# Rotary embedding on one core: which 1/32 of the data the SyncE queue carries, and how the rotation is written

## The chip, the cores and the metric

The kernel runs on one core of one Trainium2 chip. The metric is the device time of one execution in microseconds; the time quoted for a kernel is the median of its runs.

The engines that matter here are VectorE (DVE in the profile), which does all the arithmetic of the rotation, ScalarE (ACT), which evaluates the sines, GpSimd (POOL), which does no arithmetic but queues the large transfers, and SyncE (SP), which queues four small ones. TensorE (PE) is not used.

## The reference

The input `x` is float32 of shape 8 x 8 x 1024 x 64: 64 heads (batch times heads) of 1024 rows with 64 columns, 16.78 MB. Each row is rotated by angles that depend only on its position:

```python
half = x.shape[-1] // 2                     # 32
angles = np.outer(positions, freqs)         # 1024 x 32
cos, sin = np.cos(angles), np.sin(angles)
x_first, x_second = x[:, :, :, :half], x[:, :, :, half:]
out_first  = x_first * cos - x_second * sin
out_second = x_first * sin + x_second * cos
return np.concatenate([out_first, out_second], axis=-1).astype(np.float32)
```

The output is as large as the input, so an execution reads 16.78 MB and writes 16.78 MB of device memory (HBM).

## The kernel before, in words

**Tiles.** The 64 heads are cut into 8 tiles of 8 heads. A tile fills 128 partitions: partition `chunk * 8 + head` holds 64 rows (`C`) of one head, 4096 elements. The loads that GpSimd queues cast float32 to bf16 on the way in (an `xt` tile is 1 MB in on-chip memory and 2 MB in HBM); the stores that it queues cast bf16 back to float32 on the way out.

**The edge.** Two whole heads, 0 and 1 (`edge = 2`), are left out of GpSimd's transfers. SyncE loads them as float32 at the start (`xf`, L75, two transfers of 256 KB), with another layout: 8 consecutive rows (`R`) on each partition. ScalarE casts them to bf16 (`x0`, L130). Because of the other layout they need a second pair of sine and cosine tables (`sin_r`, `cos_r`), made from a second load of the positions (`pos_r`, L125). Their result `last` is float32 and leaves on SyncE's queue (L179), as the last two transfers of the program. Tile 0 therefore lacks two of its eight heads: `moves` yields six transfers of 16 partitions each for it, in and out, and its buffer is cleared first (L83) since VectorE computes on all 128 partitions.

**Loads.** GpSimd queues, in the order tile 1, tile 2, the six pieces of tile 0, tiles 3 to 6, and tile 7 in two halves of 32 rows: 14 transfers (L89). All loads have a buffer of their own. A load that is to use a completion semaphore a second time waits for the earlier transfer on it, and there are eight of them for GpSimd's transfers: the loads of tiles 3 and 4 wait for tiles 1 and 2.

**Stores held back.** A do-nothing instruction on GpSimd (L149) depends on the first half of tile 7. GpSimd's queue is in order, so no store is queued before that half has landed.

**Tables.** VectorE spreads the positions and frequencies over the partitions (L93, L94), multiplies them to turns and reduces these to less than one turn (L101 to L107); ScalarE makes `sin` and `cos` (L111 to L115) in bf16. `sin_c` has two copies per row, the second negated by VectorE (L112).

**Rotation.** Three VectorE instructions of 128 x 4096 elements per tile, in which `swap` reads the two halves of each row in exchanged order:

```python
v.tensor_mul(out=t,  in0=xt, in1=sin_c)                # L142
v.tensor_mul(out=ot, in0=xt, in1=cos_c, broadcast)     # L143
v.tensor_add(out=ot, in0=ot, in1=swap(t))              # L145
```

The scheduler puts the L142 of the next tile between L143 and L145 of a tile. In program order the tiles go 1, 0, 2, ..., 7. The tables of the edge are made after the third tile in the source; the scheduler moved their first instruction, which needs `pos_r`, ahead of the first L145. GpSimd queues a store after each tile (L155, 13 transfers).

**The end.** SyncE's two stores of the edge wait for every earlier transfer but GpSimd's last store (the `clobber_nop` list).

Of the kernel before, what the change touches and what calls it, by code (L numbers as in the profile page):

```python
# [9 lines left out]
@with_exitstack  # L10
def kernel(
    ctx: ExitStack,
    tc: tile.TileContext,
    x: bass.AP,
    freqs: bass.AP,
    positions: bass.AP,
    out: bass.AP,
):
    nc = tc.nc
    f32 = mybir.dt.float32  # L20
    bf16 = mybir.dt.bfloat16
    i32 = mybir.dt.int32
    Act = mybir.ActivationFunctionType
    Alu = mybir.AluOpType

    b, h, seq, d = x.shape
    bh = b * h
    half = d // 2
    P = 128
    twopi = 2 * math.pi  # L30
    head = seq * d

    C = 64
    R = seq // P
    chunks = seq // C
    G = P // chunks
    edge = 2  # L40
    run = C * d
    ntiles = bh // G
    assert chunks * C == seq and G * chunks == P and bh % G == 0 and R * P == seq and chunks <= 32

    singles = ctx.enter_context(tc.tile_pool(name="singles", bufs=1))
    xpool = ctx.enter_context(tc.tile_pool(name="xin", bufs=ntiles))
    opool = ctx.enter_context(tc.tile_pool(name="xout", bufs=ntiles))
    tpool = ctx.enter_context(tc.tile_pool(name="tmp", bufs=2))

    def moves(t, tile_, g, lo=0, hi=run):
        if g:
            yield (bass.AP(tensor=t.tensor, offset=t.offset + g * G * head + lo,
                           ap=[[run, chunks], [head, G], [1, hi - lo]]), tile_[:, lo:hi])
            return
        for i in range(edge, G):
            yield (bass.AP(tensor=t.tensor, offset=t.offset + i * head, ap=[[run, chunks], [1, run]]),
                   tile_[i:P:G])

    def hbm_head(t, i):
        return bass.AP(tensor=t.tensor, offset=t.offset + i * head, ap=[[R * d, P], [1, R * d]])

    v = nc.vector
    words = mybir.dt.size(positions.dtype) // 4
    const = singles.tile([P, C * words + half], i32)
    v.memset(const, 0)  # L70
    pos_i = const[:, :C * words]
    fr = const[:, C * words:].bitcast(f32)
    xf = singles.tile([P, edge, R, d], f32)
    for i in range(edge):
        nc.sync.dma_start(out=xf[:, i], in_=hbm_head(x, i))  # L75
    nc.scalar.dma_start(
        out=pos_i[0:P:G].bitcast(positions.dtype),
        in_=bass.AP(tensor=positions.tensor, offset=positions.offset, ap=[[C, chunks], [1, C]]))
    nc.scalar.dma_start(out=fr[0:P:32], in_=freqs[None, :].to_broadcast([P // 32, half]))


    xts = [xpool.tile([P, run], bf16, name="xt") for g in range(ntiles)]
    v.memset(xts[0], 0.0)  # L83
    order = [1, 0] + list(range(2, ntiles))
    for g in order:
        cuts = [0, run] if g < ntiles - 1 else [0, run // 2, run]
        for lo, hi in zip(cuts, cuts[1:]):
            for src, dst in moves(x, xts[g], g, lo, hi):
                nc.gpsimd.dma_start(out=dst, in_=src)  # L89
    half_pi = singles.tile([P, 1], f32)  # L90
    nc.gpsimd.memset(half_pi, math.pi / 2)  # L91

    v.stream_shuffle(pos_i, pos_i, [i // G * G for i in range(32)])  # L93
    v.stream_shuffle(fr, fr, [0] * 32)  # L94
    fturn = singles.tile([P, 1, half], f32)
    v.tensor_scalar_mul(out=fturn[:, 0, :], in0=fr, scalar1=1.0 / twopi)

    def tables(pos_f, n, copies, name):

        turns = singles.tile([P, n, half], f32, name=f"turns{name}")  # L100
        v.tensor_mul(out=turns, in0=pos_f.to_broadcast([P, n, half]),  # L101
                     in1=fturn.to_broadcast([P, n, half]))
        whole = singles.tile([P, n, half], f32, name=f"whole{name}")
        magic = 1.5 * 2.0 ** 23
        v.tensor_scalar(out=whole, in0=turns, scalar1=magic, scalar2=magic,  # L105
                        op0=Alu.add, op1=Alu.subtract)
        v.tensor_sub(out=turns, in0=turns, in1=whole)  # L107

        sin = singles.tile([P, n, 2, half], bf16, name=f"sin{name}")
        cos = singles.tile([P, n, copies, half], bf16, name=f"cos{name}")  # L110
        nc.scalar.activation(out=sin[:, :, 0], in_=turns, func=Act.Sin, scale=twopi)  # L111
        v.tensor_scalar_mul(out=sin[:, :, 1], in0=sin[:, :, 0], scalar1=-1.0)  # L112

        nc.scalar.activation(out=whole, in_=turns, func=Act.Abs)  # L114
        nc.scalar.activation(out=cos, in_=whole[:, :, None, :].to_broadcast([P, n, copies, half]),  # L115
                             func=Act.Sin, scale=-twopi, bias=half_pi)
        return sin, cos

    pos_f = singles.tile([P, C, 1], f32)
    v.tensor_copy(out=pos_f, in_=pos_i.rearrange("p (c w) -> p c w", w=words)[:, :, :1])  # L120
    sin_c, cos_c = tables(pos_f, C, 1, "c")


    pos_r = singles.tile([P, R, words], i32)
    tc.keep_in_program_order(nc.scalar.dma_start(  # L125
        out=pos_r.bitcast(positions.dtype),
        in_=bass.AP(tensor=positions.tensor, offset=positions.offset,
                    ap=[[R, P], [1, R], [1, 1]])))
    x0 = singles.tile([P, edge, R * d], bf16)
    tc.keep_in_program_order(nc.scalar.copy(out=x0, in_=xf.rearrange("p e r d -> p e (r d)")))  # L130

    def swap(ap):

        part, rows, pair, cols = ap.ap
        return bass.AP(tensor=ap.tensor, offset=ap.offset + half,
                       ap=[part, rows, [-half, 2], cols])

    def rotate(xt):
        flat = "p c two h -> p (c two h)"
        ot = opool.tile([P, C, 2, half], bf16, name="ot")  # L140
        t = tpool.tile([P, C, 2, half], bf16, name="t")
        v.tensor_mul(out=t.rearrange(flat), in0=xt, in1=sin_c.rearrange(flat))  # L142
        v.tensor_mul(out=ot, in0=xt.rearrange("p (c two h) -> p c two h", two=2, h=half),  # L143
                     in1=cos_c.to_broadcast([P, C, 2, half]))
        v.tensor_add(out=ot, in0=ot, in1=swap(t))  # L145
        return ot


    nc.gpsimd.keepalive_nop(ins=[nc.gpsimd.lower_ap(xts[-1][:, :run // 2])])  # L149

    stored = []
    for i, g in enumerate(order):
        ot = rotate(xts[g])
        for dst, src in moves(out, ot.rearrange("p c two h -> p (c two h)"), g):
            tc.keep_in_program_order(nc.gpsimd.dma_start(out=dst, in_=src))  # L155
        stored.append(ot)
        if i == 2:
            pos_rf = singles.tile([P, R, 1], f32)
            v.tensor_copy(out=pos_rf, in_=pos_r[:, :, :1])  # L159
            sin_r, cos_r = tables(pos_rf, R, 2, "r")  # L160

    flat = [P, edge, R * d]
    last = singles.tile(flat, f32)
    t = tpool.tile([P, C, 2, half], bf16, name="t").rearrange("p c two h -> p (c two h)")
    t = t[:, :edge * R * d].rearrange("p (n e) -> p n e", n=edge)
    for o, w in ((t, sin_r), (last, cos_r)):
        v.tensor_mul(out=o, in0=x0,  # L167
                     in1=w.rearrange("p r two h -> p (r two h)")[:, None, :].to_broadcast(flat))
    rows = "p n (r two h) -> p (n r) two h"
    v.tensor_add(out=last.rearrange(rows, two=2, h=half), in0=last.rearrange(rows, two=2, h=half),  # L170
                 in1=swap(t.rearrange(rows, two=2, h=half)))


    sp = nc.sync
    sp.keepalive_nop(ins=[sp.lower_ap(cos_r)])
    for done in [xf, const, pos_r] + stored[:-1]:
        sp.clobber_nop(outs=[sp.lower_ap(done)])
    for i in range(edge):
        tc.keep_in_program_order(sp.dma_start(out=hbm_head(out, i), in_=last[:, i]))  # L179
    sp.clobber_nop(outs=[sp.lower_ap(stored[-1])])  # L180
    for i in range(edge - 1):
        sp.clobber_nop(outs=[sp.lower_ap(last[:, i])])


# [28 lines left out]
```

## Time and profile before

| | us |
|---|---|
| median of 3 runs | 90.85 (90.83 to 91.07) |
| time of the profiled execution | 91.07 |
| its span, first to last instruction | 89.0 |
| VectorE busy | 66.6 (75%), 44 instructions |
| ScalarE busy | 9.4 (11%), 8 instructions |
| GpSimd busy (issuing transfers) | 14.2 (16%), 32 instructions |
| packets of GpSimd's queue, share of 16 DMA engines' span | 90.8% |
| HBM read / written | 16.79 MB / 16.78 MB |

The profiled execution lasted 2.07 us longer than its span: what lies before the first and after the last instruction. It was also the slowest of the three runs, 0.22 us above the median. In the page, "GB/s" counts the bytes that arrive: a load that casts to bf16 counts at half of what it reads from HBM, a store at what it writes. The share of busy time is a mean over the whole span, and the kernel has a load stage and a store stage with different limits, so it is read by stretches of time.

### The profile page before, as it was taken

The numbers are of one execution on the slowest core, as the hardware profiler recorded it, in microseconds if no ns is written. First come the engines' busy times: TensorE is split into PE (matmuls) and PEld (weight loads), VectorE is DVE, ScalarE is ACT, GpSimd is POOL, SyncE is SP. The second block draws the span as 40 slices with busy tenths as digits, with TensorE's granted clock in tenths as the row PEclk, the third lists the DMA queues.
The fourth block names the chain that finished last, engine by engine and source line by source line (L and its number), as shares of the span: only waits on it lengthen the run. The fifth ranks groups of instructions, "written<-read, shape, count | busy, mean of one in ns | idle before, by whom it ended". The sixth has DMA issues, their size and how long they took to land.

```text
span 89.0 us, 169 instructions
## 1 busy us (share of the span) xinstructions
DVE 66.6 (75%) x44; ACT 9.4 (11%) x8; POOL 14.2 (16%) x32
## 2 busy tenths in 40 slices
DVE  4414993769009679999999999999999999993000
ACT  0500006993000320000000000000000000000000
POOL 5580020650000000000961101001002002002000
DMA  2999999999999999999799999998895895899993
GB/s 23 298 159 195 217 210 214 210 203 229 216 207 221 214 214 221 203 210 195 276 354 442 435 413 449 427 420 361 354 361 228 354 376 214 354 420 405 442 351 150
DMA packets 3304, 25.45 MB, mean 286 GB/s; under 512 B 664, under 2 KB 680, under 8 KB 1448
## 3 DMA queue, kind: packets, MB, share of 16 engines
q0 software_dynamic: 2544, 24.38, 90.8%
q1 hardware_dynamic: 576, 1.05, 3.6%
q10 hardware_dynamic: 184, 0.02, 0.3%
HBM read 16.79 MB, written 16.78 MB: 377 GB/s over the span
## 4 chain that ended last, share of the span: by engine, by line
DVE 41%; DMA 34%; issue 13%; POOL 2%; DVEq 1%; POOLq 0%
DMA xt<-in_x_dram 34%; DVE ot L145 18%; DVE ot L143 17%; DVE t L142 5%; POOL xt L89 1%; DVEq L208 1%; DVE t L167 1%; POOL half_pi L91 0%; POOLq L197 0%
## 5 line engine op out<-in xcount | busy, mean ns | idle before, releaser
L143 DVE TENSOR_TENSOR ot<-xt,cosc 128x4096 bf16<-128x4096 bf16 x8 | 18.3, 2283 | 0.9 <-ACT cosc L115 0.9
L142 DVE TENSOR_TENSOR t<-xt,sinc 128x4096 bf16<-128x4096 bf16 x8 | 18.3, 2284 | 0.0
L145 DVE TENSOR_TENSOR ot<-ot,t 128x4096 bf16<-128x4096 bf16 x8 | 18.3, 2282 | 0.0
L155 POOL DMA_DIRECT2D out_dram<-ot x13 | 6.6, 512 | 54.8 <-DVE ot L145 54.8
L89 POOL DMA_DIRECT2D xt<-in_x_dram x14 | 7.3, 538 | 11.1 <-DMA xt<-in_x_dram 9.3
L159 DVE CAST pos_rf<-pos_r 128x8 f32<-128x8 int32 x1 | 0.2, 170 | 4.4 <-DMA pos_r<-in_positions_dram 4.4
L111 ACT ACTIVATE sinc<-turnsc 128x2048 bf16<-128x2048 f32 x1 | 1.9, 1909 | 10.1 <-DVE turnsc L107 10.1
L94 DVE LOAD_MASK_SELECT const<-const x1 | 0.0, 14 | 3.1 <-DMA const<-in_freqs_dram 3.1
L101 DVE TENSOR_TENSOR turnsc<-pos_f,fturn 128x2048 f32<-128x2048 f32 x1 | 2.3, 2293 | 0.0
L107 DVE TENSOR_TENSOR turnsc<-turnsc,wholec 128x2048 f32<-128x2048 f32 x1 | 2.3, 2293 | 0.0
L112 DVE TENSOR_SCALAR sinc<-sinc 128x2048 bf16<-128x2048 bf16 x1 | 0.7, 694 | 2.0 <-ACT sinc L111 2.0
L83 DVE MEMSET xt<- 128x2048 uint32 x1 | 1.8, 1765 | 0.4 <-issue 0.4
L115 ACT ACTIVATE cosc<-wholec,half_pi 128x2048 bf16<-128x2048 f32 x1 | 2.0, 2002 | 0.1
L114 ACT ACTIVATE wholec<-turnsc 128x2048 f32<-128x2048 f32 x1 | 1.9, 1895 | 0.0
L167 DVE TENSOR_TENSOR last<-x,cosr 128x1024 f32<-128x1024 bf16 x1 | 1.2, 1225 | 0.8 <-ACT cosr L115 0.8
L111 ACT ACT_TABLE_LOAD x1 | 1.3, 1283 | 2.7 <-issue 2.7
L111 ACT ACTIVATE sinr<-turnsr 128x256 bf16<-128x256 f32 x1 | 0.4, 416 | 9.3 <-DVE turnsr L107 9.3
L105 DVE TENSOR_SCALAR wholec<-turnsc 128x2048 f32<-128x2048 f32 x1 | 1.2, 1226 | 0.0
L170 DVE TENSOR_TENSOR last<-last,t 128x1024 f32<-128x1024 f32 x1 | 1.2, 1215 | 0.0
L130 ACT CAST x<-xf 128x1024 bf16<-128x1024 f32 x1 | 1.0, 1028 | 0.0
L93 DVE LOAD_MASK_SELECT const<-const x1 | 0.0, 14 | 1.2 <-DMA const<-in_positions_dram 1.2
L70 DVE MEMSET const<- 128x160 int32 x1 | 0.2, 192 | 0.8 <-PEq L197 0.8
(16 smaller groups left out, 4.5 us busy)
## 6 DMA issues: line engine op xcount, KB each, us to landing
out_dram<-ot POOLq DMA_DIRECT2D x7, 2048.0 KB, 6.8
xt<-in_x_dram POOLq DMA_DIRECT2D x6, 1024.0 KB, 13.7
out_dram<-ot POOLq DMA_DIRECT2D x6, 256.0 KB, 7.6
xt<-in_x_dram POOLq DMA_DIRECT2D x2, 512.0 KB, 24.5
xt<-in_x_dram POOLq DMA_DIRECT2D x6, 128.0 KB, 13.5
xf<-in_x_dram SPq DMA_DIRECT2D x2, 256.0 KB, 2.9
out_dram<-last SPq DMA_DIRECT2D x2, 256.0 KB, 5.6
const<-in_positions_dram ACTq DMA_DIRECT2D x1, 8.0 KB, 3.2
```

Source lines behind the costliest of these rows:

```text
L83: v.memset(xts[0], 0.0)
L89: nc.gpsimd.dma_start(out=dst, in_=src)
L101: v.tensor_mul(out=turns, in0=pos_f.to_broadcast([P, n, half]), in1=fturn.to_broadcast([P, n, half]))
L107: v.tensor_sub(out=turns, in0=turns, in1=whole)
L111: nc.scalar.activation(out=sin[:, :, 0], in_=turns, func=Act.Sin, scale=twopi)
L114: nc.scalar.activation(out=whole, in_=turns, func=Act.Abs)
L115: nc.scalar.activation(out=cos, in_=whole[:, :, None, :].to_broadcast([P, n, copies, half]), func=Act.Sin, scale=-twopi, bias=half_pi)
L142: v.tensor_mul(out=t.rearrange(flat), in0=xt, in1=sin_c.rearrange(flat))
L143: v.tensor_mul(out=ot, in0=xt.rearrange("p (c two h) -> p c two h", two=2, h=half), in1=cos_c.to_broadcast([P, C, 2, half]))
L145: v.tensor_add(out=ot, in0=ot, in1=swap(t))
L155: tc.keep_in_program_order(nc.gpsimd.dma_start(out=dst, in_=src))
L167: v.tensor_mul(out=o, in0=x0, in1=w.rearrange("p r two h -> p (r two h)")[:, None, :].to_broadcast(flat))
```

## The change

The edge is cut differently, and with it the rotation is written in another way.

- SyncE no longer carries two whole heads. It loads the first 16 rows of every partition of tile 0 at the start (`x0`, two transfers of 8 rows, 256 KB each) and stores the last 16 rows of every partition of tile 7 at the end (two transfers of 256 KB). The bytes are as many as before; each of the 128 pieces of a transfer is 2 KB, as before, but they lie 16 KB or more apart in HBM where they used to be contiguous.
- The layout is now the same for all data, so the second tables, `pos_r` and the buffer clearing of tile 0 go away. ScalarE casts the early rows straight into tile 0's buffer, ahead of the sines.
- GpSimd's loads are 9 (tile 0 without its first 16 rows, tiles 1 to 6, tile 7 in two halves), its stores 8 (tile 7 without its last 16 rows).
- The sine table has one copy and no negated half; both tables are broadcast. The addition with `swap` is replaced by a subtraction and an addition on half rows.
- The do-nothing instruction that holds GpSimd's stores back until the first half of tile 7 has landed, and the two halves of tile 7, are in both kernels.

The diff, cut to its core:

```diff
-    half = ...; edge = 2; R = seq // P
-    def moves(t, tile_, g, lo=0, hi=run): ...
-    def hbm_head(t, i): ...
+    def hbm(t, g, lo=0, hi=C):
+        return bass.AP(tensor=t.tensor, offset=t.offset + g * P * run + lo * d,
+                       ap=[[run, chunks], [seq * d, group], [1, (hi - lo) * d]])
...
-    xf = singles.tile([P, edge, R, d], f32)
-    for i in range(edge):
-        nc.sync.dma_start(out=xf[:, i], in_=hbm_head(x, i))
+    piece = 8
+    head = 2 * piece
+    x0 = singles.tile([P, head, d], f32)
+    for r in range(0, head, piece):
+        nc.sync.dma_start(out=x0[:, r:r + piece], in_=hbm(x, 0, r, r + piece))
...
-    v.memset(xts[0], 0.0)
-    order = [1, 0] + list(range(2, ntiles))
-    for g in order:
-        cuts = [0, run] if g < ntiles - 1 else [0, run // 2, run]
+    for g in range(ntiles):
+        cuts = [0 if g else head, C] if g < ntiles - 1 else [0, C // 2, C]
         for lo, hi in zip(cuts, cuts[1:]):
-            for src, dst in moves(x, xts[g], g, lo, hi):
-                nc.gpsimd.dma_start(out=dst, in_=src)
+            nc.gpsimd.dma_start(out=xts[g][:, lo:hi], in_=hbm(x, g, lo, hi))
...
-        v.tensor_scalar_mul(out=sin[:, :, 1], in0=sin[:, :, 0], scalar1=-1.0)
...
-    pos_r = singles.tile([P, R, words], i32)
-    tc.keep_in_program_order(nc.scalar.dma_start(out=pos_r..., in_=...))
-    tc.keep_in_program_order(nc.scalar.copy(out=x0, in_=xf...))
+    nc.scalar.copy(out=xts[0][:, :head], in_=x0)
...
-        v.tensor_mul(out=t.rearrange(flat), in0=xt, in1=sin_c.rearrange(flat))
-        v.tensor_mul(out=ot, in0=xt..., in1=cos_c.to_broadcast([P, C, 2, half]))
-        v.tensor_add(out=ot, in0=ot, in1=swap(t))
+        v.tensor_mul(out=t, in0=xt, in1=sin_h[:, lo:hi, None, :].to_broadcast(pair))
+        v.tensor_mul(out=ot, in0=xt, in1=cos_h[:, lo:hi, None, :].to_broadcast(pair))
+        v.tensor_sub(out=ot[:, :, 0], in0=ot[:, :, 0], in1=t[:, :, 1])
+        v.tensor_add(out=ot[:, :, 1], in0=ot[:, :, 1], in1=t[:, :, 0])
...
-        if i == 2:
-            pos_rf = singles.tile([P, R, 1], f32)
-            v.tensor_copy(out=pos_rf, in_=pos_r[:, :, :1])
-            sin_r, cos_r = tables(pos_rf, R, 2, "r")
...
+    tail = 2 * piece
+    for g in [1, 0] + list(range(2, ntiles)):
+        hi = C if g < ntiles - 1 else C - tail
+        ot = opool.tile([P, C, d], bf16, name="ot")[:, :hi]
+        rotate(g, 0, hi, ot)
+        tc.keep_in_program_order(nc.gpsimd.dma_start(out=hbm(out, g, 0, hi), in_=ot))
+    last = singles.tile([P, tail, d], f32)
+    rotate(ntiles - 1, C - tail, C, last)
...
-    for i in range(edge):
-        tc.keep_in_program_order(sp.dma_start(out=hbm_head(out, i), in_=last[:, i]))
+    for r in range(0, tail, piece):
+        lo = C - tail + r
+        tc.keep_in_program_order(
+            sp.dma_start(out=hbm(out, ntiles - 1, lo, lo + piece), in_=last[:, r:r + piece]))
```

On the engines, the changed program has these instructions where the two differ. VectorE: per tile 128 x 4096 twice and 128 x 2048 twice, in the order "next tile's sine product, subtraction, addition, next tile's cosine product"; the last tile as 48 rows and 16 rows. ScalarE: the cast of the early rows with an activation table load ahead of it, another table load, then the three activations. GpSimd: nine loads of which only the ninth waits (for tile 0's load), then eight stores.

## The prediction

> **What bounds the kernel now.** I read the 40 slices first, because the mean shares (VectorE 75%, GpSimd's queue 90.8%) hide the stages.
>
> ```profile
> DVE  4414993769009679999999999999999999993000
> ...
> DMA  2999999999999999999799999998895895899993
> GB/s 23 298 159 195 217 210 214 210 203 229 216 207 221 214 214 221 203 210 195 276 354 442 435 413 449 427 420 361 354 361 228 354 376 214 354 420 405 442 351 150
> ```
>
> A slice is 2.2 us. Up to slice 19 the transfers are loads, at about 213 GB/s arriving as bf16, so 426 read. From slice 20 they are stores. The DMA row is full until slice 27, then shows 8s and 5s with VectorE at 9: transfers wait for arithmetic. The windows give the rates (columns: window and length; busy of DVE, ACT, POOL with counts; clock; DMA share; GB/s).
>
> ```profile
> 11.00:42.00 31.00, 22.27 (x17) 8.09 (x7) 3.25 (x6) 1.00 1.04 213
> ...
> 42.40:43.40 1.00, 1.00 (x1) 0.00 (x0) 1.00 (x2) 1.00 0.32 66
> 43.40:60.40 17.00, 17.00 (x9) 0.00 (x0) 3.48 (x8) 1.00 1.07 427
> 60.40:80.40 20.00, 20.00 (x11) 0.00 (x0) 1.88 (x4) 1.00 0.84 333
> ```
>
> Stores run at 427 GB/s while finished tiles lie ready, and at 333 once VectorE delivers one tile (2.10 MB) per 6.6 us. From 60 us to the end VectorE is the bound. So the question is why it is late, and the timeline tells.
>
> ```profile
> 19.98 2.29 DVE L143 TENSOR_TENSOR ot<-xt,cosc 128x4096 bf16<-128x4096 bf16 x1 [0.88 <-ACT cosc L115]
> 26.70 0.17 DVE L159 CAST pos_rf<-pos_r 128x8 f32<-128x8 int32 x1 [4.43 <-DMA pos_r<-in_positions_dram]
> 26.78 2.28 DVE L145 TENSOR_TENSOR ot<-ot,t 128x4096 bf16<-128x4096 bf16 x1
> ...
> 42.40 3.41 POOL L155 DMA_DIRECT2D out_dram<-ot  x7 [23.13 <-DVE ot L145]
> ...
> 79.72 1.22 DVE L170 TENSOR_TENSOR last<-last,t 128x1024 f32<-128x1024 f32 x1
> 80.09 0.52 POOL L155 DMA_DIRECT2D out_dram<-ot  x1 [4.48 <-DVE ot L145]
> 81.90 2.32 SPq L179 DMA_DIRECT2D out_dram<-last  x2
> ```
>
> VectorE starts rotating at 16.81, stands still for 4.43 us on the small load `pos_r`, then works without a hole worth naming to 80.94 (79.72 + 1.22). The first store, at 42.40, is blamed on "DVE ot"; but tile 1's `ot` was done at 29.06 (26.78 + 2.28). What held it is L149: the first half of tile 7, queued at 18.18, needed 23.5 us and landed at 41.7.
>
> **What the Trainium skill says.** *VectorE: DVE Perf Modes*, "The perf-mode tier table": a bf16 `tensor_tensor` takes two elements a cycle, 1224 ns for 2048; float32 one, 2293 ns. The trace agrees: 2293 for f32 128x2048 (L101), 2283 for bf16 128x4096. *DMA: Bandwidth & Descriptors*, "Anatomy of one DMA": about 2.0 us plus bytes / 436e3; for 2.10 MB that is an estimate of 6.8 us, and the unobstructed stores at 61.87, 68.48, 75.08 and 80.09 took 6.7 to 6.8. The same page, "Queues, rings and completion order": each DMA engine goes round its queues packet by packet. That fits `pos_r`, 8 KB in 128 rows, at 8.7 us under the load stream, against 3.2 for the first position load ahead of it.
>
> **The change part by part.**
>
> *VectorE, start.* The clearing of tile 0 (L83, 1.77 us) goes, two small memsets come (about 0.2 each). Cost nothing: VectorE waits afterwards for `freqs` until 7.8 anyway (3.10 us before L94). The turns end at 14.1 as before, the sine at 14.14 + 1.91 = 16.05; the negation (L112, 0.69) goes, so the first product starts near 16.1, not 16.81. It needs tile 1, now second in the queue: 0.52 + 1.57 + 2.10 = 4.2 MB must be in. Before, tiles 1 and 2 and the edge, 4.7 MB, were in when GpSimd's wait for tile 2 ended at 16.27; 0.5 MB at 426 less gives about 15. The margin is thin, 1 us.
>
> *VectorE, middle.* The `pos_r` wait (4.43) goes, and with it the second tables: 1.8 us of VectorE (L159, L101, L105, L107, L112) and 1.3 of waits on ACT (0.48 + 0.83).
>
> *VectorE, per tile.* Before 3 x 2.20 (start to start) = 6.60. Now two at 2.20 and two at 128x2048. No such row is in the trace; by the two bf16 rows, 2283 for 4096 and 681 for 1024, I interpolate 1215 ns (the skill's 1224 agrees); started 0.08 apart less, 1.14. So 2 x 2.20 + 2 x 1.14 = 6.68. Full tiles: 7. Tile 7's 48 rows: 2 x 1.67 + 2 x 0.88 = 5.1. The last 16: 0.61 (the L167 bf16 row), 1.14 (L167 f32), two f32 halves of L170 at about 0.6 each: 2.95. Sum 46.8 + 5.1 + 2.95 = 54.8; VectorE ends near 16.1 + 54.8 = 70.9, ten us earlier. The sine product with a broadcast table replaces a flat one; L143 has the same broadcast and takes 2283, L142 2284: nothing.
>
> *ScalarE.* The cast moves ahead of the sines with two table loads: 1.28 + 1.03 + 1.28 = 3.6 us after the early rows land (0.74 + 2.9 and a second piece, about 4.1): done by 7.7, hidden under the wait until 14.1. If that cover were gone the sine would be late, and the first product with it. Its edge activations (1.5 us) go, off the path.
>
> *GpSimd.* 5 loads and 5 stores fewer, 10 x 0.52 = 5.2 us. Hidden: the stream is full while it issues. Eight loads go out from about 1.3 to 5.6 with no wait; the ninth, the second half of tile 7, waits for tile 0 (about 10 us) and is needed at 42. Queued behind it is only the held-back first store. Eight stores need no semaphore that is still in flight.
>
> *SyncE.* Same count and bytes. Its end stores wait for tile 6's store, as they now wait for the last store but one. The pieces are scattered; no row prices that. Bounds: nothing, to the 2 us of the final stretch again (262 GB/s from 86 to 88 halved). A gain is excluded[...]. I take nothing.
>
> *The path afterwards.* The loads carry the same bytes, so I keep the first store at 42.40. The stretch from 4 to 7 us ran at 159 instead of 213, 0.76 us lost while GpSimd issued small pieces; GpSimd issues then in the new kernel too, so I keep the loss, and put its absence into the range. From 42.40 the stores have VectorE ahead: tiles 1, 0, 2 ready by 38.3, tile 3 at 45, then one per 6.68, tile 7 at 68.5. The stream takes one per 4.9 us and comes to tile 7 near 77: 8 us of slack. So the end is the sum of the bytes. First store landed at 42.40 + 7.1 = 49.5. Then 16.78 - 2.10 - 0.52 = 14.16 MB at 430 (427 in the shown window, 433 from 50 to 55; the slower one holds the six pieces that go away): 32.9, so 82.4. SyncE's pair ends 1.15 after GpSimd's last store, as now (issued at 82.25 and 5.8 to land, 88.05; against 80.09 + 6.8 = 86.9): 83.55; to the end of the span 0.95 as now: **84.5**, against 89.0. With the 2.07 around the span 86.57; the profiled execution was 0.22 above the median, so **86.4**.
>
> **Rivals.**
> *The write rate sags* over 39 us without a pause. For: 64 to 66 and 84 to 86 show 393, 60 to 62 shows 410. Against: 17 us at 427, and these windows have gaps of supply. At 410, 14.16 MB takes 34.5: 88.0; at 393, 36.0: 89.5; it equals the old time at 378 or so.
> *VectorE becomes the bound again, and slower.* If the half-row operations with rows of 32 elements ran at one element a cycle, each would take 2.29 as f32 does, 2.20 start to start: 8.8 per tile, 7 x 8.8 + 6.7 = 68.3, tile 7 ready at 84.4; its store about 5.7 (1.57 MB / 430 + 2.0), the pair 1.15 more, 0.95 to the end: 92.2, time 94. VectorE binds from some 8 us more, 1.2 per tile, and the whole is slower than before from 12.4 more, 1.8 per tile. Against: L145 reads its second operand in exchanged rows of 32 at 2282, and L112 writes every second row of 32 at full rate (694).
> *The tables come late.* If `freqs` takes the 8.7 us of `pos_r`, everything shifts 2.7, inside the slack: still 86.4.
> *It does not do what it says.* The halved last load and the held-back store are in both kernels. If only they mattered and the rest traded evenly, 90.85.
>
> **How the numbers follow.** About 0.3% (0.27 us) is what a measurement of this kernel can tell from no change. Forecast 0.80 (the late tables included), sagging rate 0.10, of which 0.01 lands at no change, an even trade 0.03, VectorE at one element 0.07. Faster 0.89, same 0.04, slower 0.07. Range: down 0.76 for the early loss and 0.5 for 433 and better, 85.1; up 1.9 for scattered pieces or 410, 88.3.
>
> **What would show it.** Right: no DVE idle after 16 us above 1, first store near 42.4, DMA row full to the end with stores at 430, VectorE done near 71, SyncE's pair near 79. Wrong: 128x2048 rows at 2.2 us; a first store later than 43; a store window below 410 while `ot` tiles lie ready.

## The result and the profile after

The changed kernel takes **85.35 us** (median; 85.31 to 85.44) against 90.84 for the kernel before: a ratio of 0.9395, 95% interval 0.9374 to 0.9417. Forecast were 86.4 us and a range of 85.1 to 88.3. The profiled execution lasted 85.34 us with a span of 83.5, so 1.84 lie around the span. Several of the kernels below, all of them with transfers of 16 partitions, have some runs 1 to 2.5 us above their others; the ratios leave such runs out, the medians do not.

The 40 slices of the changed kernel (one is 2.1 us): VectorE without a gap from slice 8 (counted from 0) to its end in slice 34, and the DMA row full from slice 1 to the last but one. The 8s and 5s are gone.

```profile
DVE  1025994099999999999999999999999999200000
...
DMA  0999999999999999999999999999999999999991
GB/s 0 191 224 235 237 220 208 224 208 212 216 220 220 212 224 204 216 202 214 216 369 400 408 439 432 432 439 408 463 400 447 432 432 432 408 471 396 424 384 68
```

The windows of the changed kernel, columns as before. From 60.4 to 80.4 the stores now run at 428 GB/s, where they ran at 333; the change from loads to stores (42.4 to 43.4) carries 500 where it carried 66; and the window from 4 to 7, whose loss the forecast kept (159), shows 215.

```profile
4.00:7.00 3.00, 0.51 (x3) 0.00 (x0) 1.55 (x3) 1.00 1.01 215
11.00:42.00 31.00, 27.90 (x17) 9.31 (x6) 0.58 (x2) 1.00 1.03 214
42.40:43.40 1.00, 1.00 (x2) 0.00 (x0) 0.59 (x2) 1.00 1.26 500
43.40:60.40 17.00, 17.00 (x11) 0.00 (x0) 1.57 (x3) 1.00 1.05 425
60.40:80.40 20.00, 11.10 (x11) 0.00 (x0) 1.05 (x2) 1.00 1.06 428
```

The timeline of the changed kernel (start, length, engine, line, operation). The early rows reach ScalarE only at 10.99; the first rotation product follows at 16.58; the first store goes out at 41.41; tile 6's store at 65.35; tile 7's at 69.36; VectorE ends at 71.53 (70.85 + 0.68); SyncE's pair is queued at 77.60.

```profile
10.99 1.28 ACT L103 ACT_TABLE_LOAD   x1 [10.99 <-DMA x<-in_x_dram]
...
16.58 4.49 DVE L113 TENSOR_TENSOR t<-xt,sin_h 128x4096 bf16<-128x4096 bf16 x2 [3.07 <-ACT sin_h L98]
...
41.41 1.58 POOL L128 DMA_DIRECT2D out_dram<-ot  x3 [31.78 <-DVE ot L114]
...
65.35 0.52 POOL L128 DMA_DIRECT2D out_dram<-ot  x1 [5.62 <-DVE ot L116]
69.36 0.52 POOL L128 DMA_DIRECT2D out_dram<-ot  x1 [3.49 <-DVE ot L116]
...
70.85 0.68 DVE L116 TENSOR_TENSOR last<-last,t 128x512 f32<-128x512 f32 x1
77.60 1.23 SPq L141 DMA_DIRECT2D out_dram<-last  x2
```

Its transfers (KB each, median us from issue to landing). A full store now takes 13.4 us to land where an unobstructed one took 6.8: the stores queue up and wait for the DMA engines, where before these waited for VectorE.

```profile
out_dram<-ot POOLq DMA_DIRECT2D x7, 2048.0 KB, 13.4
...
x<-in_x_dram SPq DMA_DIRECT2D x2, 256.0 KB, 6.6
out_dram<-last SPq DMA_DIRECT2D x2, 256.0 KB, 4.4
```

### The profile page after: what moved, and what is told of

Read it like the earlier page. It is cut to its first block, busy times and chain, and to the rows that moved or that the text cites. A ratio compares the mean times of both kernels' runs of the same rounds, so it can differ in the third digit from the quotient of the medians.

```text
span 83.5 us, 151 instructions
## 1 busy us (share of the span) xinstructions
DVE 61.8 (74%) x48; ACT 9.3 (11%) x6; POOL 9.2 (11%) x21
## 3 DMA queue, kind: packets, MB, share of 16 engines
q1 hardware_dynamic: 576, 1.05, 4.1%
## 4 chain that ended last, share of the span: by engine, by line
DVE 53%; issue 12%; DMA 11%; ACT 7%; SPq 1%; DVEq 1%; ACTq 0%
DVE ot L114 20%; DMA x<-in_x_dram 11%; DVE t L113 11%; DVE ot L116 11%; DVE ot L115 8%; ACT sin_h L98 2%; ACT L98 2%; ACT L103 2%; DVE last L114 1%; ACT xt L103 1%; DVE last L115 1%; SPq L56 1%; DVEq L170 1%; ACTq L103 0%
## 5 line engine op out<-in xcount | busy, mean ns | idle before, releaser
L113 DVE TENSOR_TENSOR t<-xt,sin_h 128x4096 bf16<-128x4096 bf16 (+2 forms) x9 | 18.3, 2045 | 3.1 <-ACT sin_h L98 3.1
L114 DVE TENSOR_TENSOR ot<-xt,cos_h 128x4096 bf16<-128x4096 bf16 (+1 forms) x8 | 17.6, 2216 | 0.0
L128 POOL DMA_DIRECT2D out_dram<-ot x8 | 4.2, 525 | 56.1 <-DVE ot L114 31.8
L115 DVE TENSOR_TENSOR ot<-ot,t 128x2048 bf16<-128x2048 bf16 (+1 forms) x8 | 9.5, 1183 | 0.0
L116 DVE TENSOR_TENSOR ot<-ot,t 128x2048 bf16<-128x2048 bf16 (+1 forms) x8 | 9.5, 1182 | 0.0
L76 POOL DMA_DIRECT2D xt<-in_x_dram x9 | 4.8, 573 | 4.4 <-DMA xt<-in_x_dram 3.6
L89 DVE TENSOR_TENSOR turns<-pos_f,fturn 128x2048 f32<-128x2048 f32 x1 | 2.3, 2293 | 0.0
L95 DVE TENSOR_TENSOR turns<-turns,whole 128x2048 f32<-128x2048 f32 x1 | 2.3, 2293 | 0.0
L101 ACT ACTIVATE cos_h<-whole,half_pi 128x2048 bf16<-128x2048 f32 x1 | 2.0, 2002 | 0.0
L98 ACT ACTIVATE sin_h<-turns 128x2048 bf16<-128x2048 f32 x1 | 1.9, 1909 | 0.0
L100 ACT ACTIVATE whole<-turns 128x2048 f32<-128x2048 f32 x1 | 1.9, 1893 | 0.0
L114 DVE TENSOR_TENSOR last<-xt,cos_h 128x1024 f32<-128x1024 bf16 x1 | 1.2, 1215 | 0.0
## 6 DMA issues: line engine op xcount, KB each, us to landing
out_dram<-ot POOLq DMA_DIRECT2D x7, 2048.0 KB, 13.4
out_dram<-ot POOLq DMA_DIRECT2D x1, 1536.0 KB, 11.8
```

The source lines that it names most:

```text
L76: nc.gpsimd.dma_start(out=xts[g][:, lo:hi], in_=hbm(x, g, lo, hi))
L89: nc.vector.tensor_mul(out=turns, in0=pos_f.to_broadcast([P, C, half]), in1=fturn.to_broadcast([P, C, half]))
L95: nc.vector.tensor_sub(out=turns, in0=turns, in1=whole)
L98: nc.scalar.activation(out=sin_h, in_=turns, func=Sin, scale=twopi)
L100: nc.scalar.activation(out=whole, in_=turns, func=mybir.ActivationFunctionType.Abs)
L101: nc.scalar.activation(out=cos_h, in_=whole, func=Sin, scale=-twopi, bias=half_pi)
```

## The experiments

**1. One move in the kernel before: `pos_r` queued early.**

```diff
     nc.scalar.dma_start(out=fr[0:P:32], in_=freqs...)
+    pos_r = singles.tile([P, R, words], i32)
+    nc.scalar.dma_start(out=pos_r..., in_=positions...)
...
-    tc.keep_in_program_order(nc.scalar.dma_start(out=pos_r..., in_=positions...))
```

> The kernel before with one move: the small load pos_r is queued on ScalarE's queue ahead of the two table loads instead of under the load stream; the edge tables, the two whole heads, the six pieces and the three-instruction rotation stay. Theory (VectorE was late, the rest is the sum of the bytes): no 4.4 us wait, VectorE ends near 75, the stores run at about 427 GB/s to the end, time near 86.5 with the early ramp loss kept. Rival (the two whole heads or the rotation as such cost the time, the late start only hides it): VectorE ends earlier but the time stays near 90.8.

Measured: runs at 84.96, 85.34, 86.45 and 87.20; ratio to the kernel before 0.936 (0.926 to 0.945). Its timeline: the cast of `pos_r` runs at 8.02, and VectorE ends at 74.15 (72.93 + 1.22), 6.8 us earlier than in the kernel before.

```profile
8.02 0.16 DVE L159 CAST pos_rf<-pos_r 128x8 f32<-128x8 int32 x1
...
40.54 3.93 POOL L155 DMA_DIRECT2D out_dram<-ot  x8 [23.10 <-DMA xt<-in_x_dram]
...
72.93 1.22 DVE L170 TENSOR_TENSOR last<-last,t 128x1024 f32<-128x1024 f32 x1
```

Its windows: the store rate stays at 424 to the end.

```profile
4.00:7.00 3.00, 0.31 (x2) 0.11 (x1) 2.37 (x5) 1.00 1.05 213
...
43.40:60.40 17.00, 17.00 (x9) 0.00 (x0) 2.13 (x5) 1.00 1.07 427
60.40:80.40 20.00, 13.75 (x8) 0.00 (x0) 1.57 (x3) 1.00 1.05 424
```

In two of its four runs this single move brings the whole gain (84.96 and 85.34 against 85.35); the other two, at 86.45 and 87.20, keep 1.1 and 1.85 less of it. The two whole heads, the second tables, the six pieces, the clearing of tile 0 and the three-instruction rotation are all still there. The rival that those cost the time, so that it would stay near 90.8, falls in all four runs. In this profile the first store also came 1.86 us earlier than in the kernel before (40.54 against 42.40); what sets that time is the subject of experiments 4 and 5.

**2 and 3. How much VectorE time the changed kernel has to spare.**

```diff
         ots.append(ot)
+        if g == 0:
+            idle = singles.tile([P, C, half], f32)
+            for _ in range(2):      # 5 in the other kernel
+                tc.keep_in_program_order(nc.vector.tensor_mul(out=idle, in0=turns, in1=turns))
```

> The changed kernel with two float32 128x2048 products added on VectorE after the first two tiles, 4.4 us, as much as the pos_r wait had taken. Theory (slack): by the changed kernel's trace tile 6 is stored 5.4 us earlier than the stream needs it (queued at 65.35, landed at 77.52, an unobstructed store takes 6.8), so nothing moves: 85.35 within 0.3. Rival (VectorE still sets the end): 85.35 + 4.4 = 89.8.

> The same with five such products, 11 us. Theory (slack of 5.4 us at tile 6): 11 - 5.4 = 5.6 more, 91.0, and the gaps of supply come back in the store stage. Rival (slack of 8 us, as the prediction had it): 85.35 + 3 = 88.4. Rival (VectorE sets the end already): 96.4.

Measured: 85.56 (85.50 to 85.72) with 4.4 us added and 91.81 (91.38 to 92.12) with 11. Tile 6's store and the late window, first with two products, then with five:

```profile
70.30 0.52 POOL L132 DMA_DIRECT2D out_dram<-ot  x1 [5.62 <-DVE ot L116]
```

```profile
60.40:80.40 20.00, 16.04 (x14) 0.00 (x0) 1.57 (x3) 1.00 1.06 428
```

```profile
76.34 0.52 POOL L132 DMA_DIRECT2D out_dram<-ot  x1 [5.62 <-DVE ot L116]
```

```profile
60.40:80.40 20.00, 20.00 (x16) 0.00 (x0) 1.62 (x4) 1.00 0.83 328
```

With 4.4 us the store is queued 4.95 later (70.30 against 65.35; the sine was half a microsecond later too), just inside the 5.4 that the stream leaves, and the rate is untouched. With 11 it is queued 10.99 later, the rate falls to 328 and the median rises by 6.5 us, 0.9 more than expected: the slack is 4.5 by the medians (4.9 by the two profiled executions, 91.41 and 85.34). Both rivals, 8 us of slack and none, fall.

**4 and 5. Where the first store's microsecond went.** The forecast kept the first store at 42.40; it came at 41.41. I asked whether the pieces of tile 0 cost it, in both directions: pieces put into the changed kernel, and the kernel before profiled once more.

```diff
-    for g in range(ntiles):
-        cuts = [0 if g else head, C] ...
+    for g in [1, 2, 0] + list(range(3, ntiles)):
+        if g == 0:
+            for i in range(group):
+                nc.gpsimd.dma_start(out=xts[0][i:P:group, head:], in_=<rows 16 to 63 of head i>)
+            continue
```

> The changed kernel with tile 0 loaded as before: after tiles 1 and 2, in pieces of 16 partitions (eight, since no whole head is left out), same bytes. Theory (the small pieces, while GpSimd queues them, cost the early loads their rate): the window from 4 to 7 us falls from 215 to about 160 GB/s, the first store comes 0.7 to 1 us later than 41.41, time near 86.3. Rival (the clearing of tile 0 or the whole heads made the loss): 215 stays, time 85.35.

> The kernel before, profiled once more. The prediction took its window from 4 to 7 us (159 GB/s) as a property of the kernel and kept the 0.76 us it costs in the forecast; with pos_r queued early, pieces and clearing unchanged, the same window showed 213. If the loss belongs to the kernel as it is written, 159 comes back and the first store is again near 42.4; if it belongs to that one execution, the window shows some 213 and the first store comes near 41.4, with the span about 0.4 to 1 us shorter.

Measured: 85.93, 85.96, 86.05 and 88.41 with the pieces, so 0.6 us more than the changed kernel in the lower three. The early window does not fall (222), and the first store comes 0.25 later, not 0.7 to 1; I have not followed where the rest of the 0.6 goes.

```profile
4.00:7.00 3.00, 0.51 (x3) 0.00 (x0) 1.36 (x3) 1.00 1.04 222
```

```profile
41.66 1.58 POOL L135 DMA_DIRECT2D out_dram<-ot  x3 [22.45 <-DVE ot L123]
```

The kernel before, profiled again (91.33 us), has no early loss in that window either by its mean rate (208), and yet its first store comes at 42.72, after a change-over that carries 12 GB/s:

```profile
4.00:7.00 3.00, 0.31 (x2) 0.03 (x1) 2.37 (x5) 1.00 1.03 208
...
42.40:43.40 1.00, 1.00 (x1) 0.00 (x0) 0.68 (x2) 1.00 0.06 12
```

```profile
42.72 3.41 POOL L155 DMA_DIRECT2D out_dram<-ot  x7 [23.13 <-DVE ot L145]
```

So the pieces as such do not cost the early loads their rate, and the theory fell. The mean rate of that window does not tell when the first store comes either. The trace's completion marks do. A load is complete when its sixteen parts have all landed. The parts of tile 7's first half landed from 39.98 to 41.73 in the kernel before and from 39.56 to 42.05 when it was profiled again, against 39.96 to 40.74 in the changed kernel, 39.45 to 39.87 in experiment 1 and 40.65 to 40.98 in experiment 4. In each of the five the first store is queued 0.67 or 0.68 us after the last part. In the kernel before a few late parts (five, and then a single one) hold the store back, while the other DMA engines run out of loads: that is the change-over at 66 and at 12 GB/s.

Those parts are as late in tile 1's load, the first that GpSimd queues: eleven landed by 9.59 and five from 10.73 on in the kernel before, fifteen by 9.27 and one at 11.42 in its second profile. The records of single packets (the units in which the trace records what a DMA engine moves) show the start of it. They do not name the engine, but each begins close to the end of the one before it, so that they can be sorted into sixteen chains. In the kernel before, the first packet of eleven chains begins between 3.56 and 3.86 and takes 0.62 to 0.66 us; that of the other five begins between 4.30 and 4.65 and takes 1.66 to 1.82. In the second profile fifteen begin by 3.85 and take 0.62, and one begins at 4.81 and takes 2.04. In experiment 1 all sixteen begin by 3.97 and take at most 0.78. So the delay is made in the window from 4 to 7 after all, in the first packets of the stream; where one engine of sixteen is late, the mean of the window hardly shows it.

Why some engines begin late is open. GpSimd queues the pieces at that time (3.46 to 6.37), but it does so at the same time in experiment 1, which has no such lag; and the first part of the first piece landed only at 14.9, long after tile 1, so moving the pieces cannot have made it. The four kernels that load pieces of 16 partitions scatter from run to run (the kernel before 90.25 to 92.92 over 23 runs, experiment 1 by 2.2 us, experiment 4 by 2.5, experiment 8 below by 2.4), and the kernels without them lie within 0.3 except the one bound by VectorE (0.7). That is a tie that was seen, not a cause that was shown.

**6. SyncE's end stores without their wait for the other stores.**

```diff
-    for done in [x0, pos_i, fr] + ots[:-1]:
-        sp.clobber_nop(outs=[sp.lower_ap(done)])
+    act = nc.scalar
+    for done in [x0, pos_i, fr] + ots[:-1]:
+        act.clobber_nop(outs=[act.lower_ap(done)])
```

> The changed kernel in which SyncE's two end stores wait only for their own data; the waits for the earlier transfers move to ScalarE, which is idle by then. Theory (the end is the sum of the bytes, and the pair at the very end is written slower than the stream, about 300 against 427 GB/s): the pair is queued near 72 and mixes with the stores of tiles 6 and 7, 0.5 to 0.7 us less, time near 84.7. Rival (the 2 KB pieces cost their time wherever they lie): 85.35. Rival (they delay the large stores by more than they save): 85.6 or more.

Measured: 85.42 (85.27 to 85.47), no gain. The pair was queued 6 us earlier, at 71.65, and took 10.4 us to land instead of 4.4:

```profile
71.65 1.24 SPq L142 DMA_DIRECT2D out_dram<-last  x2
```

```profile
out_dram<-last SPq DMA_DIRECT2D x2, 256.0 KB, 10.4
```

It landed when it had landed before (82.13 and 82.61 us, against 82.12 and 82.61), the last of all. Its first packet moved only at 78.19, and then it did mix with tile 7's store, whose last part landed at 81.94 instead of 81.18. From 78 to 80 the two queues moved almost the same number of packets (q0 is GpSimd's, q1 SyncE's; then packets, MB and their share of the 16 DMA engines' time):

```profile
q0 software_dynamic: 58, 0.71, 86.1%
q1 hardware_dynamic: 54, 0.11, 19.6%
```

SyncE's packets of 2 KB took 0.116 us each there and GpSimd's of 12 KB 0.473, so a byte of the pair took half as long again as a byte of tile 7. That and the time (85.42) fit the rival of the 2 KB pieces.

**7. No hold on the stores**, once more beside the changed kernel on one chip.

```diff
-    nc.gpsimd.keepalive_nop(ins=[nc.gpsimd.lower_ap(xts[-1][:, :C // 2])])
```

> The changed kernel without the do-nothing instruction on GpSimd that holds the stores back until the first half of tile 7 has landed; tile 7 is still loaded in two halves. Theory (sum of the bytes): the first store is queued near 27.7 behind all loads, the drop of the rate at the change from loads to stores (295 GB/s from 42 to 43) goes, 0.4 to 0.8 us less, time near 84.8. Rival (stores taking turns with loads slow both): 85.35 or more. Rival (the early stores push the last loads back so that VectorE runs short): above 86.

> The changed kernel itself, on the same chip as the two versions beside it: 85.35 within 0.2.

> The changed kernel without the hold, once more and beside the changed kernel on one chip. If the 0.17 us seen before (85.18 against 85.35 on another occasion) is the hold's, the two differ again by 0.1 to 0.3 us; if it was the occasion, they agree within 0.1.

Measured: 85.18 (85.16 to 85.24), and on the second occasion 85.18 (85.15 to 85.27) beside 85.35 (85.14 to 85.44) for the changed kernel. The first store is queued at 27.98, the stretch from 42 to 43 carries 373 GB/s (first fence, without the hold) instead of 295 (second, changed kernel), and the later rate is as before. The 0.17 us came twice, and only one of ten runs of the changed kernel (85.14) lies below 85.18; the theory's 0.4 to 0.8 us was missed. Neither rival shows: VectorE never ran short of loads. By these 0.2% it is the fastest of the steady versions.

```profile
27.98 0.54 POOL L127 DMA_DIRECT2D out_dram<-ot  x1 [18.43 <-DVE ot L116]
```

```profile
42.00:43.00 1.00, 1.00 (x1) 0.00 (x0) 0.00 (x0) 1.00 1.19 373
43.40:60.40 17.00, 17.00 (x11) 0.00 (x0) 1.57 (x3) 1.00 1.06 432
```

```profile
42.00:43.00 1.00, 1.00 (x1) 0.00 (x0) 0.99 (x2) 1.00 0.86 295
```

**8. Whole heads, `pos_r` early, no hold**: both single moves in the kernel before.

> The kernel before with pos_r queued early and without the instruction that holds GpSimd's stores back: whole heads on SyncE's queue, as before. Theory (the late start was the whole loss, the rest is the sum of the bytes; whole heads give a quicker start of the loads): with pos_r early alone the first store came at 40.54 and the span was 82.7 in the undisturbed profile; without the hold the dip of the rate at the change from loads to stores goes, 0.2 less, time near 84.8, below the changed kernel. Rival (the new cut of the edge is worth something by itself): 85.3 or more.

Measured: 85.23, 85.25, 85.41, 86.92, 87.40 and 87.62, ratio 0.940 (0.935 to 0.946) against 0.940 (0.936 to 0.944) for the changed kernel beside it. The theory's 84.8 was missed, and the lower group lies at the rival's "85.3 or more". Without the hold in both, whole heads give 85.23 to 85.41 in that group and the new cut 85.15 to 85.27 (experiment 7): in time the two cuts are equal to 0.2 us. Half of the runs with whole heads lie 1.5 us and more above that; the new cut is steadier.

**9. The early rows in one transfer.**

```diff
-    for r in range(0, head, piece):
-        nc.sync.dma_start(out=x0[:, r:r + piece], in_=hbm(x, 0, r, r + piece))
+    for r in range(0, head, head):
+        nc.sync.dma_start(out=x0[:, r:r + head], in_=hbm(x, 0, r, r + head))
```

> The changed kernel with its early rows in one transfer of 512 KB (4 KB pieces) instead of two of 256 KB (2 KB pieces). In the changed kernel the second transfer landed 9.3 us after it was queued, behind packets of the load stream, and the early bytes came slower than in the kernel before (115 against 377 GB/s from 2.5 to 3 us). Theory (small scattered pieces cost the start): the early rows land before 8 us, ScalarE's table load starts by then, the first store comes 0.3 to 0.5 us earlier, time near 85.0. Rival (the bytes are the same, the order within the load stage doesn't matter): first store at 41.4 and 85.35.

Measured: 85.91 (85.89 to 85.93), 0.5 us slower. The early rows do land sooner, and the cast runs at 6.18; the table load ahead of it no longer waits for them (2.70). But the first store comes at 41.92:

```profile
2.70 1.28 ACT L103 ACT_TABLE_LOAD   x1 [2.70 <-issue]
6.18 1.04 ACT L103 CAST xt<-x 128x1024 bf16<-128x1024 f32 x1 [2.19 <-DMA x<-in_x_dram]
```

```profile
41.92 1.58 POOL L128 DMA_DIRECT2D out_dram<-ot  x3 [31.47 <-DMA xt<-in_x_dram]
```

The theory fell. The sooner sine is worth nothing, since VectorE has slack; why the loads end half a microsecond later is open (the marks of tile 7's first half spread over 1.1 us here, 40.16 to 41.24).

## Why the prediction was right, and where it was off

- **What bounds the kernel.** Right: VectorE was late, not overloaded. Experiment 1 takes the `pos_r` wait alone away and gets the whole gain in its two lower runs; experiments 2 and 3 show that afterwards VectorE is off the path by about 5 us. The wait itself was as the prediction read it: from 23 to 26 us in the kernel before, the load stream (q0) and ScalarE's queue with `pos_r` (q10) moved the same number of packets. The first packet of `pos_r` moved 3.4 us after it was queued, and then its 128 packets of 64 bytes, eight for each of the sixteen DMA engines, went one for one with load packets of 0.62 us: an estimate of 5.0 us. The two make 8.4 of the 8.7 us.

```profile
q0 software_dynamic: 83, 0.64, 101.7%
q10 hardware_dynamic: 83, 0.00, 4.0%
```

- **VectorE's sum.** The bf16 128x2048 operations took 1215 to 1216 ns against 1215 interpolated; 54.8 us of work was forecast and 54.95 done (16.58 to 71.53). The second tables' five instructions sum to 1.5 us and not 1.8; no later number rests on that. The rival of one element a cycle falls with that row.
- **ScalarE's step was mis-sized.** I had the early rows in by 4.1 and the cast hidden. The second of the two transfers took 9.5 us, ScalarE began at 10.99, the sine at 14.64 instead of 14.14, the first product at 16.58 instead of 16.1. The cover that I named was used up. That only half a microsecond showed is luck: the angles were ready at 13.51 and not at 14.1, because `freqs` came 0.6 sooner, so the cast cost 1.1. The slack took it.
- **The slack was mis-sized.** Tile 6 is nearer than tile 7: 5.4 us by the trace (landed 77.52, less 6.8, less 65.35) and 4.5 to 4.9 by experiment 3. At tile 7 it is 6.1 and not 8 (landed 81.18, less the prediction's 5.7 for this store, less 69.36): the 8 was counted from tile 7 being ready to the stream's arrival, without the time that a store takes beyond its bytes, 1.9 us by an estimate from the unobstructed stores (6.8 less 2.10 MB at 430 GB/s).
- **"I keep the first store at 42.40" was the step that failed**, by 0.99 us, nearly all of the 1.05 between forecast and result. It kept 0.76 us of early loss because GpSimd issues in the new kernel too. The window shows 215 there, and 213 and 222 in experiments 1 and 4, which issue small pieces: issuing alone does not bring the loss. What held the first store of the kernel before was five late parts in each load, from five DMA engines that began the stream late; in the changed kernel the parts land within 0.8 us. The range had this case in it. Why engines begin late stays open.
- **The store stage.** 14.16 MB in 32.9 us was forecast. The first store landed at 48.4 (41.41 + 7.0), GpSimd's last at 81.2 (69.36 + 11.8): 32.8. The sagging rate falls.
- **The end.** The pair landed 1.4 after GpSimd's last store (82.6), 0.25 more than forecast, out of a bound of 2 us for scattered pieces. The 0.9 to the end of the span and the 1.84 around it are as forecast (0.95, and 2.07 less 0.22).
- **That it does not do what it says.** This rival falls. The words about the halved load and the held-back store describe both kernels; doing without the hold is worth 0.17 us.

## What to carry to other kernels

A small load that an engine needs in mid-program should be queued before the large stream starts, not when it is wanted: here 8 KB queued under the stream took 8.7 us, and queueing them early took 3.8 to 6 us off a 91 us kernel. When a profile shows a transfer-bound stage with gaps, ask which engine supplies it and when that engine started, before counting its work. And compute the slack for every tile, not only for the last.

## What the runs showed of the hardware that I had not expected

- A small transfer can be slow beside a large one for two reasons. It takes turns with it packet by packet, whatever the packets' sizes: 83 against 83 packets for `pos_r` (23 to 26 us, kernel before), 54 against 58 for the pair in experiment 6. The Trainium skill (*DMA: Bandwidth & Descriptors*, "Queues, rings and completion order") has each engine go round its queues packet by packet; the trace agrees. Turns of equal packets are not equal shares of the rate: the pair's 2 KB stood against 12 KB. And its first packet starts late: 3.4 us after queueing for `pos_r`, 6.5 for the pair, against 2.7 for the pair in the changed kernel, queued when most of the stream was out. Why is open.
- The completion of a load is set by its slowest sixteenth: the parts of one 1 MB transfer landed up to 2.5 us apart, and in that execution the distance was the same at the first tile (8.92 to 11.42) and the last (39.56 to 42.05). A loss of one DMA engine at 5 us was still there at 42.
- One transfer of 512 KB in 4 KB pieces at the start was 0.5 us worse for the whole than two of 256 KB in 2 KB pieces (experiment 9), though it landed sooner itself (6.16 against 10.92 us).
